# A decoder step on one core: the second layer norm's variance from sums taken per token during the mixing projection, and the modulated input as one product plus a low-rank matmul

## The chip, the cores and the metric

One Trainium2 chip; the program runs on 1 of its cores. The metric is device microseconds of one execution, as the median of several runs. The profile is of one further execution, in which a hardware profiler recorded every instruction. Engine names are those of the profile: PE (matmul), PEld (its weight loads), DVE (VectorE), ACT (ScalarE), POOL (GpSimd), SP (which issues the weight loads from memory). Each engine takes its own instructions strictly in the order in which the program wrote them, and an instruction that waits holds all those behind it on its engine.

## The reference

One layer for 288 tokens (256 of a prompt and 8 sequences of 4) with 2048 features. The change touches the stretch between the output projection of the mixing half and the up-projection of the channel half:

```
mod = silu(c) @ w_ada + b_ada
sh1, sc1, g1, sh2, sc2, g2 = split(mod, 6)
u   = layernorm(x) * (1 + sc1) + sh1
...                                   # convolution group and mLSTM group, concatenated into y
mix = y @ w_out
x   = layernorm(ALPHA * x + (1 + g1) * mix) * ln1_g + ln1_b
u2  = layernorm(x) * (1 + sc2) + sh2
a, g = split(u2 @ w_up, 2)
y   = silu(dwconv3(a)) * g
x   = layernorm(ALPHA * x + (1 + g2) * (y @ w_down)) * ln2_g + ln2_b
```

So two layer norms follow each other: the one that ends the mixing half, with gain ln1_g and bias ln1_b, and at once the one that opens the channel half. c has 9 rows: one for the prompt, one for each short sequence.

## The kernel before

**Layout.** Features lie on the 128 partitions and tokens along the free axis: an activation is 16 tiles (`xa[0]` to `xa[15]`) of 128x288. A weight matrix comes as 128x128 blocks, 16 to an item of 1 MB. ACT rounds each half of an item to `whi` and DVE subtracts to get `wlo` (helper `split_to`, L299 and L312); activations are split in the same way, and each product is three matmuls (`mm3`, L455 to L457). `next_block` asks for the half that is two halves ahead (`LOOK`). At most 7 items are held (`RAWB`).

**Items.** `plan` writes out the order of the items: weight items and, in between, items of `w_ada` that PE multiplies with silu(c) (`ada_item`, L366, tile `adaps`): 16 of them for each of the four vectors G1, SC2, SH2 and G2. The last vector, G2, is not needed before the down-projection; 13 of its items stand between the mixing projection and the up-projection, three later.

**Side work.** `side` starts a generator that is stepped by `tick`, once for each weight block; a `yield n` lets n blocks pass. It fixes the place of its instructions among the others on every engine at the time the program is built.

**Mixing projection.** Sixteen output tiles (tile `mix`, 48 matmuls each). The old `x` arrives by 16 loads that POOL issues one by one, each followed at once by a multiplication with ALPHA that waits for it (L1054 and L1055). After each tile `residual` (L1179 to L1183, DVE) adds the gated result. `TileNorm` with the name `ln1` takes the statistics of the first norm: after 11 tiles PE makes a shift from their sum, DVE and POOL subtract it, ACT squares, POOL adds up, and DVE adds up the tiles weighted with ln1_g (L1094).

**Between the projections.** Three matmuls with a matrix of ones give mean, mean square and weighted sum; then each tile is centred, scaled and squared again by DVE, POOL and ACT in an order that `Plan.run` works out from due times, and sixteen more matmuls (L1217, tile `var`) give the second variance. `rstd_of` (Ln and Exp on ACT, three DVE steps) gives the second scale. Then each tile is modulated (`u2_hi`, `u2_lo`), split, and used by the first six up-projection tiles (`pss`, 96 blocks).

**Later.** POOL brings `x1` back to its unscaled form beside the up-projection (`restore`, L1307 and L1308).

Of the kernel before, what the change touches and what calls it, by code (L numbers as in the profile page):

```python
# [36 lines left out]
U2_DVE = 2  # L37
SPLITS = (1, 3)
BIAS_AHEAD = 3
LN1_POOL = {1, 3, 5, 7, 9, 11, 13}  # L40
# [4 lines left out]
G2_EARLY = 13  # L45
G2_WAIT = 8
# [24 lines left out]
def plan():  # L71
# [66 lines left out]
    items += mix(rest[n:], w)  # L138
# [40 lines left out]
def constants():  # L179
# [17 lines left out]
    return dict(ident=ident, causal=causal, causal_s=causal_s, ind=ind, ind96=ind96, sel=sel, pick=pick)  # L197


def body(tc, d, off, items, blocks):  # L200
# [4 lines left out]
    with ctx:  # L205
# [50 lines left out]
        live = [0]  # L256
        barrier = [len(items)]
# [813 lines left out]
        class TileNorm:  # L1071


            def __init__(self, name, base, w=None):
# [5 lines left out]
                self.w = w  # L1080
                self.wsum = None

            def centre(self, m):
# [5 lines left out]
                if self.w is not None:  # L1089
                    if self.wsum is None:  # L1090
                        self.wsum = st(self.name + "w")
                        V.tensor_scalar(self.wsum, x, self.w[:, m:m + 1], None, ALU.mult)
                    else:
                        V.scalar_tensor_tensor(self.wsum, x, self.w[:, m:m + 1], self.wsum, ALU.mult, ALU.add)  # L1094
# [68 lines left out]
            def finish(self):  # L1163
# [25 lines left out]
        ngb = pers.tile([P, 1], F32, name="ngb")  # L1189
        V.tensor_scalar(ngb, gbm[:, 0:1], -1.0, None, ALU.mult)  # L1190
        bb1 = pers.tile([P, KB], F32, name="bb1")
        V.tensor_scalar(bb1, b1v, gbm[:, 1:2], None, ALU.subtract)

        ln1 = TileNorm("ln1", xa, g1v)
        for m in range(KB):
            ps = aps("mix")
            for k in range(KB):
# [4 lines left out]
            ln1.add(m, xa[m])  # L1202
        y = None
        steps = ln1.finish()
        drain(ada_done[len(GROUPS) + 1])
        drain(ada_done[len(GROUPS) + 2])
        x1 = xa
        var_ps = mps("var1", N)
        rstd1, mean = ln1.rstd, ln1.mean
        wp = st("wp")  # L1210
        done = []

        def scaled(E, k):
            E.tensor_tensor(x1[k], x1[k], rstd1, ALU.mult)
            q = st("sq1")
            A.activation(q, x1[k], AF.Square, bias=bb1[:, k:k + 1])
            T.matmul(var_ps, ones, q, start=(not done), stop=(len(done) == KB - 1))  # L1217
            done.append(k)

        next(steps)  # L1220
        pl = Plan()
        w = pl.op("v", VC, lambda E: V.scalar_tensor_tensor(wp, mean, ngb, ln1.psW, ALU.mult, ALU.add), at=0.6)
        r = ()
        for i in range(3):
            r = (pl.op("v", VC, lambda E: next(steps), deps=r, wait=LAT, at=0.9, stage=9),)
        pend = []
        for k in range(KB):
            e, c = ("g", GC) if k in LN1_POOL else ("v", VC)
            a = pl.op(e, c, lambda E, k=k: E.tensor_tensor(x1[k], x1[k], mean, ALU.subtract))
            b = pl.op("v", VC, lambda E, k=k: V.scalar_tensor_tensor(x1[k], x1[k], g1v[:, k:k + 1], wp,  # L1230
                                                                  ALU.mult, ALU.subtract),
                      deps=(a, w), wait=LAT)
            pend.append((k, e, c, b))
        for k, e, c, b in pend:
            pl.op(e, c, lambda E, k=k: scaled(E, k), deps=(b,) + r, wait=LAT, stage=1)
        pl.run()
        ln1 = None
        barrier[0] = len(items)
        var = st("var1")
        V.tensor_scalar(var, var_ps, EPS, None, ALU.add)  # L1240
        while items[pos[0]][0] == "a":
            take()
        rstd = rstd_of(var, "rstd1")

        def biased(k):
            A.activation(x1[k], x1[k], AF.Identity, bias=bb1[:, k:k + 1])

        for k in range(U2_DVE, U2_DVE + BIAS_AHEAD):
            biased(k)
        A.preload_act_table(AF.Silu)  # L1250
        def conv_state(n):
# [4 lines left out]

        sf_next = conv_state(0)
        u2 = [None] * KB
        hold = {}
        pss = [aps("up") if i < 3 else mps("up", N) for i in range(KOUT)]  # L1260

        def u2_hi(k):
            t = st("u2t")
            if k < U2_DVE:
                V.scalar_tensor_tensor(t, x1[k], bb1[:, k:k + 1], rstd, ALU.add, ALU.mult)
            else:
# [267 lines left out]
```

## Time and profile before

| | |
|---|---|
| time, median of 3 runs | 1553.33 us (1552.72 to 1553.34) |
| the profiled execution's own time | 1552.51 us |
| its span in the trace | 1550.6 us |
| granted PE clock, mean over the span | 0.991 |
| PE busy | 1510.7 us, 97% |
| DVE / ACT / POOL busy | 938.4 / 592.5 / 293.5 us |
| chain that ended last, by engine | PE 89%, DVE 8%, issue 1%, ACT 1% |
| mixing projection, first to last matmul | 517.9 to 639.8 us |
| first six up-projection tiles | 675.3 to 718.2 us |

PE's share is an average over stages. The place that the change rewrites is short: between 639.8 us and 675.3 us no weight block of a projection is multiplied. A row of the trace's timeline gives the start in us from the span's start, the duration, the engine, the line of the code, the operation with output and input tiles and shapes, how many like it are merged, and in brackets how long the engine had been idle and what ended that.

### The profile page before, as it was taken

To read this page: it belongs to the slowest core of one execution; us is meant where nothing else is said; L and a number is where in the kernel's file an instruction comes from. 1 tells how busy PE (TensorE), PEld (TensorE's weight loads), DVE (VectorE), ACT (ScalarE), POOL (GpSimd) and SP (SyncE) were. 2 spreads that over 40 slices of the span, in tenths; PEclk is the share of its full clock that TensorE was granted. 3 is DMA by queue.
4 is the path that set the end of the run, shared out by engine and by line. 5 is a ranking of instruction groups with operands and counts; after the bars stand their busy time and mean duration, and the time that the engine had idled before them with its cause. 6 is when DMAs were issued, how large, how long until landed. Compare 5 with 4: busy or idle time off the path is not lost.

```text
span 1550.6 us, 28061 instructions
## 1 busy us (share of the span) xinstructions
PE 1510.7 (97%) x11692; PEld 1409.7 (91%) x11692; DVE 938.4 (61%) x1643; ACT 592.5 (38%) x877; POOL 293.5 (19%) x502
## 2 busy tenths in 40 slices
PE   8999999999999999989999999999999999999994
PEld 7988988888888888569999999999999999999994
DVE  5566566777764446887655545555555445555557
ACT  5533234422234323355443333344443334444334
POOL 2320005210112234534530000000000000000235
PEclk9999999999999999999999999999999999999997
DMA  9887777569899876765545444444445444444401
GB/s 390 326 348 289 296 272 271 191 224 338 329 373 322 296 291 242 315 248 198 190 180 190 171 163 167 160 163 164 165 171 187 163 163 163 164 163 167 163 29 61
DMA packets 49614, 343.72 MB, mean 222 GB/s; under 512 B 5872, under 2 KB 6384, under 8 KB 9040
## 3 DMA queue, kind: packets, MB, share of 16 engines
q1 hardware_dynamic: 46656, 329.08, 57.1%
q0 software_dynamic: 2688, 12.68, 2.1%
q8 instruction: 91, 1.49, 0.4%
q14 instruction: 35, 0.29, 0.0%
q10 hardware_dynamic: 144, 0.19, 0.0%
HBM read 329.61 MB, written 12.31 MB: 221 GB/s over the span
## 4 chain that ended last, share of the span: by engine, by line
PE 89%; DVE 8%; issue 1%; ACT 1%; POOL 0%; DMA 0%; SPq 0%; DVEq 0%; ACTq 0%; POOLq 0%
PE g L456 6%; PE a L455 6%; PE g L455 6%; PE a L456 6%; PE g L457 6%; PE a L457 6%; PE dn L457 5%; PE dn L455 5%; PE dn L456 5%; PE adaps L366 5%; PE h L455 5%; PE h L456 4%; PE h L457 4%; PE mix L455 2%; DVE wlo L312 2%; PE mix L456 2%
## 5 line engine op out<-in xcount | busy, mean ns | idle before, releaser
L299 ACT CAST whi<-raw 128x1024 fp32r<-128x1024 f32 x410 | 424.1, 1046 | 435.2 <-PE dn L457 160.4
L312 DVE TENSOR_TENSOR wlo<-raw,whi 128x1024 fp32r<-128x1024 f32 x410 | 508.0, 1254 | 59.3 <-ACT whi L299 58.8
L457 PE MATMUL dn<-y2h,whi 128*128 128x288 f32 x704 | 208.0, 295 | 0.0
L455 PE MATMUL dn<-y2l,whi 128*128 128x288 f32 x704 | 207.5, 295 | 0.0
L456 PE MATMUL dn<-y2h,wlo 128*128 128x288 f32 x704 | 207.0, 294 | 0.0
L456 PE MATMUL g<-u2h,wlo 128*128 128x288 f32 x656 | 194.5, 297 | 0.0
L455 PE MATMUL a<-u2l,whi 128*128 128x288 f32 x656 | 194.1, 296 | 0.0
L455 PE MATMUL g<-u2l,whi 128*128 128x288 f32 x656 | 194.0, 296 | 0.0
L457 PE MATMUL g<-u2h,whi 128*128 128x288 f32 x656 | 193.7, 295 | 0.0
L457 PE MATMUL a<-u2h,whi 128*128 128x288 f32 x656 | 193.4, 295 | 0.0
L456 PE MATMUL a<-u2h,wlo 128*128 128x288 f32 x656 | 193.2, 295 | 0.0
L455 PE MATMUL h<-ul,whi 128*128 128x288 f32 x512 | 156.3, 305 | 4.4 <-DVE ul L581 1.6
L456 PE MATMUL h<-uh,wlo 128*128 128x288 f32 x512 | 152.2, 297 | 0.0
L457 PE MATMUL h<-uh,whi 128*128 128x288 f32 x512 | 151.8, 296 | 0.0
L455 PEld LDWEIGHTS dn<-y2l,whi 128*128 128x128 f32 x704 | 132.3, 188 | 0.1
L1016 POOL COPY fnew<-hal 128x2 f32<-128x2 f32 x44 | 9.7, 220 | 648.0 <-ACT hal L1328 648.0
L457 PEld LDWEIGHTS dn<-y2h,whi 128*128 128x128 f32 x704 | 132.2, 188 | 0.0
L456 PEld LDWEIGHTS dn<-y2h,wlo 128*128 128x128 f32 x704 | 132.0, 188 | 0.1
L455 PEld LDWEIGHTS a<-u2l,whi 128*128 128x128 f32 x656 | 123.4, 188 | 2.5 <-issue 2.5
L456 PEld LDWEIGHTS a<-u2h,wlo 128*128 128x128 f32 x656 | 123.5, 188 | 0.0
L455 PEld LDWEIGHTS g<-u2l,whi 128*128 128x128 f32 x656 | 123.4, 188 | 0.0
L456 PEld LDWEIGHTS g<-u2h,wlo 128*128 128x128 f32 x656 | 123.3, 188 | 0.0
(392 smaller groups left out, 2926.1 us busy)
## 6 DMA issues: line engine op xcount, KB each, us to landing
raw<-wst SPq DMA_DIRECT2D x300, 1024.0 KB, 4.9
raw<-cst SPq DMA_DIRECT2D x8, 1024.0 KB, 5.4
cs_o<-raw POOLq DMA_DIRECT2D x8, 1024.0 KB, 10.8
xa<-xT POOLq DMA_DIRECT2D x16, 144.0 KB, 5.4
xin<-xT SPq DMA_DIRECT2D x5, 432.0 KB, 5.6
y_o<-yout SPq DMA_DIRECT2D x4, 432.0 KB, 2.4
cp_o<-cnew POOLq DMA_DIRECT2D x8, 128.5 KB, 6.8
raw<-wst SPq DMA_DIRECT2D x2, 512.0 KB, 13.9
```

What stands on the lines that cost most here:

```text
L299: A.copy(his[n], raws[i][:, hf * 1024:(hf + 1) * 1024])
L312: V.tensor_tensor(lo, r, hi.bitcast(F32), ALU.subtract)
L366: T.matmul(ps[32 * s:32 * s + 32, 0:n], csil[:, k, :], r[:, c0:c0 + n], start=(k == 0), stop=(k == 15))
L455: T.matmul(ps, hi, ul, start=start, stop=False)
L456: T.matmul(ps, lo, uh, start=False, stop=False)
L457: T.matmul(ps, hi, uh, start=False, stop=stop)
L1016: G.tensor_copy(dst[:, 0, :], hal[:, NP:NP + 2])
```

## The change

**Statistics.** All sums that the two norms need are taken while the mixing projection runs. With z the shifted tile, six sums over the features are needed per token: z, z², (ln1_g z)², and z weighted with ln1_g, with -2 ln1_g² and with 2 ln1_g times the centred bias. The shift comes from the first 4 tiles (`S1`) in place of 11. For each tile ACT makes two squares, DVE three weighted running sums (`accumulate`), POOL three plain ones (`gather`).

**Steps with tokens on partitions.** The running sums are the left operand of matmuls with a column of ones (`sums`), so that 128 tokens lie on partitions and the sums of all 288 tokens are a 128x3 array. Both variances, both scales and the coefficients are then worked out on 128x3 arrays (`sv`).

**u2.** It is written as x1 times one factor per feature and token, plus a product of a coefficient matrix (`cft`, from `coefficients`, made while the projection runs) with a matrix `tok` that holds per-token values in 27 rows and zeros and ones in others; both are split in two parts for precision. The factor is spread over the partitions by matmuls with the identity (`tokens`). The constant rows of `tok` are a new input, loaded by POOL and cast by ACT ahead of the mixing projection.

**Order.** 6 items of G2 (`G2_EARLY`) stand between the projections and 10 within the up-projection; the last 6 weight items of the mixing projection (`MIX_LAST`) have no w_ada item between them. The first half of the up-projection's weights is split during the last mixing tile (`UP_AT`), four of the six sums are taken there too (`SUMS_AT`). `restore` takes three POOL operations per tile in place of two.

```diff
-U2_DVE = 2
-SPLITS = (1, 3)
-BIAS_AHEAD = 3
-LN1_POOL = {1, 3, 5, 7, 9, 11, 13}
+S1 = 4
+G2_FIRST = 4
+CF_AT = 4
+SUMS_AT = 10
+UP_AT = 9
 LN2_ROLES = "vgvvgvgvvgvgvvvd"
 STORES = [(0,), (1, 2), (3, 4, 5), (6, 7, 8), (9, 10, 11), (12, 13, 14), (15,)]
 RES0 = 8
 RES1 = 12
-G2_EARLY = 13
-G2_WAIT = 8
+G2_EARLY = 6
+MIX_LAST = 6
...
-    items += mix(rest[n:], w)
+    items += mix(rest[n:], w[:-MIX_LAST]) + w[-MIX_LAST:]
...
+        bb1, gg, gbb, ngg2, gbb2, gs, ng = (gb[:, i] for i in range(7))
         V.tensor_scalar(bb1, b1v, gbm[:, 1:2], None, ALU.subtract)
-
-        ln1 = TileNorm("ln1", xa, g1v)
+        V.tensor_tensor(gg, g1v, g1v, ALU.mult)
+        V.tensor_tensor(gbb, g1v, bb1, ALU.mult)
+        V.tensor_scalar(ngg2, gg, -2.0, None, ALU.mult)
...
+        for j, v in enumerate((gg, gbb2, gb[:, 7])):
+            V.tensor_tensor(tmp3[:, j, 0:8], v[:, 0:8], v[:, 8:16], ALU.add)
+            for n in (4, 2, 1):
+                V.tensor_tensor(tmp3[:, j, 0:n], tmp3[:, j, 0:n], tmp3[:, j, n:2 * n], ALU.add)
+        ps = mps("gbm3", 3)
+        T.matmul(ps, ones, tmp3[:, :, 0], start=True, stop=True)
+        cst = pers.tile([P, 6], F32, name="cst")
+        V.tensor_copy(cst[:, 0:3], ps)
...
+        tok = st("tok", F32R)
+        t = st("tok0")
+        nc.gpsimd.dma_start(out=t, in_=d["tok"])
+        A.copy(tok, t)
+        tt = st("tt", F32R)
+        G.memset(tt.bitcast(F32), 0.0)
...
+        def squares(m):
+            q, p = st("ln1q"), st("ln1p")
+            A.activation(q, xa[m], AF.Square)
+            A.activation(p, xa[m], AF.Square, scale=g1v[:, m:m + 1])
+            return q, p
+
+        def stats(m):
+            q, p = squares(m)
+            z = xa[m]
+            for name, w in (("w", g1v), ("x", ngg2), ("b", gbb2)):
+                accumulate(name, z, w[:, m:m + 1])
+            acc1["n"] = m
+            gather("q", q)
+            gather("p", p)
+            gather("z", z)
+
+        def first_stats(total):
+            A.preload_act_table_set("natural_log_exp_and_others")
+            yield 4
+            ps = mps("shift1", N)
+            T.matmul(ps, ones, total, start=True, stop=True)
+            sh = st("shift1")
+            A.activation(sh, ps, AF.Copy, scale=2048.0 / (P * S1))
+            for m in range(S1, KB):
+                G.tensor_tensor(xa[m], xa[m], sh, ALU.subtract)
+            yield 1
+            for m in range(S1):
+                V.tensor_tensor(xa[m], xa[m], sh, ALU.subtract)
+                stats(m)
+                yield 2
...
+            F = rawp.tile([P, 2048], F32, tag="r", name=nm("cf"))
+            G.memset(F, 0.0)
...
+                A.copy(Cv[:, ks, 0:27], D[h][:, :, 0:27])
+                A.copy(Cv[:, ks, 96:105], D[h][:, :, 27:36])
+                A.copy(Cv[:, ks, 64:91], D[h][:, :, 0:27])
...
+                V.tensor_tensor(Cv[:, ks, 32:59], D[h][:, :, 0:27], F[:, ks, 0:27], ALU.subtract)
+                V.tensor_tensor(Cv[:, ks, 105:114], D[h][:, :, 27:36], F[:, ks, 96:105], ALU.subtract)
...
+            for q in range(4):
+                ps = mps("cft")
+                for k in range(4):
+                    T.transpose(ps[:, k * P:(k + 1) * P], F[:, 4 * q + k, :], ident)
+                for k in range(2):
+                    t = st("cft", F32R)
+                    A.copy(t[:, 0:256], ps[:, 256 * k:256 * k + 256])
...
+            for i, (a, b) in enumerate(BLK):
+                T.matmul(stp[bank][:, 8 * i + c:8 * i + c + w], x[:, a:b], rhs, start=start and i == 0,
+                         stop=stop and i == 2)
+
+        def late_sums():
+            yield SUMS_AT
+            for name, c in (("w", 1), ("x", 2), ("b", 3), ("p", 5)):
+                sums(name, acc1[name], c)
+
+        def up_split():
+            yield UP_AT
+            barrier[0] = len(items)
+            split_to(upcoming_w())
...
+            elif m < KB - 1:
+                if m == S1:
+                    drain(fs)
+                stats(m)
...
-        steps = ln1.finish()
-        drain(ada_done[len(GROUPS) + 1])
-        drain(ada_done[len(GROUPS) + 2])
-        x1 = xa
-        var_ps = mps("var1", N)
-        rstd1, mean = ln1.rstd, ln1.mean
-        wp = st("wp")
-        done = []
-
-        def scaled(E, k):
-            E.tensor_tensor(x1[k], x1[k], rstd1, ALU.mult)
-            q = st("sq1")
-            A.activation(q, x1[k], AF.Square, bias=bb1[:, k:k + 1])
-            T.matmul(var_ps, ones, q, start=(not done), stop=(len(done) == KB - 1))
-            done.append(k)
...
+        q, p = squares(KB - 1)
+        sums("z", acc1["z"], 0)
+        sums("q", acc1["q"], 4)
+        sums("lin", xa[KB - 1], 0)
+        sums("q", q, 4, True)
+        sums("p", p, 5, True)
...
+        V.tensor_tensor(Rr, r1, r2, ALU.mult)
+        r2b = sv[:, :, 10:11].to_broadcast([P, 3, 27])
+        V.tensor_tensor(tt[:, :, 0:27], tp3, r2b, ALU.mult)
+        V.tensor_tensor(tt[:, :, 32:59], tp3, r2b, ALU.mult)
+        V.tensor_tensor(tp3, tp3, r2b, ALU.mult)
+        V.tensor_tensor(tt[:, :, 64:91], tp3, ttf[:, :, 0:27], ALU.subtract)
...
+        for _ in range(G2_FIRST):
+            if items[pos[0]][0] == "a":
+                take()
+        rps = mps("rr", N)
+        tokens(rps, spread(11), P)
+        R = st("R")
+        A.copy(R, rps)
+        tps = mps("tokp", N)
+        tokens(tps, lambda i: ttf[:, i, 0:96], 96)
+        A.copy(tok[0:96], tps[0:96])
...
+        def u2_t(k):
+            t = st("u2t")
+            V.scalar_tensor_tensor(t[:, 0:NP], x1[k][:, 0:NP], gs[:, k:k + 1], R[:, 0:NP], ALU.mult, ALU.mult)
+            V.tensor_tensor(t[:, NP:N], x1[k][:, NP:N], R[:, NP:N], ALU.mult)
+            V.tensor_tensor(smp(t), smp(t), bc_t(fsv[:, k]), ALU.mult)
+            hold[k] = t
+        def u2_corr(k):
+            cps[k] = mps("corr", N)
+            T.matmul(cps[k], cft[k // 2][:, (k % 2) * P:(k % 2 + 1) * P], tok, start=True, stop=True)
...
+            V.tensor_tensor(t, t, cps.pop(k), ALU.add)
...
+        for k in range(KB):
+            for i, p in enumerate(pss):
+                mm3(p, next_block(), u2[k], k == 0, k == KB - 1)
+                if i == KOUT // 2 - 1 and k + 2 < KB:
+                    u2_corr(k + 2)
+                    u2_hi(k + 2)
+                    if k + 3 < KB:
+                        u2_t(k + 3)
+                    u2_lo(k + 2)
...
+                G.tensor_tensor(x1[k], x1[k], rb[0], ALU.mult)
+                G.tensor_tensor(x1[k], x1[k], rb[1], ALU.subtract)
+                G.tensor_scalar(x1[k], x1[k], ga[:, 0, k:k + 1], ga[:, 1, k:k + 1], ALU.mult, ALU.add)
```

The order of the built program shows the change at three places. The numbers in the names count buffers. First, ACT at the start of the mixing projection, before: the gate of the last o tile (`sg`), its split (`yh`), then weight halves.

```order
L299 CAST whi_5996<-raw_5828 128x1024
L1064 ACTIVATE sg_6013<-o_5935 128x288
L462 CAST yh_6016<-sg_6013 128x288
L299 CAST whi_6046<-raw_5828 128x1024
L299 CAST whi_6076<-raw_5900 128x1024
```

And ACT at the same place now, where `tok` is the new table and `whi_6009` and `whi_6096` are the two weight halves of the second mixing tile:

```order
L312 CAST whi_6009<-raw_5885 128x1024
L1077 ACTIVATE sg_6026<-o_5961 128x288
L475 CAST yh_6029<-sg_6026 128x288
L1228 CAST tok_6069<-tok_1032_6070 128x288
L312 CAST whi_6096<-raw_5885 128x1024
L312 CAST whi_6126<-raw_5966 128x1024
```

One instruction is new on ACT: the cast of the loaded table stands ahead of the second tile's second weight half. The load that it reads is on POOL's queue; POOL, from the last two of the 16 loads of x on, now:

```order
L1067 DMA xa_5407<-xT 128x288
L1068 TENSOR_SCALAR xa_5407<-xa_5407 128x288
L1067 DMA xa_5410<-xT 128x288
L1068 TENSOR_SCALAR xa_5410<-xa_5410 128x288
L1227 DMA tok_1032_6070<-tok 128x288
L1230 MEMSET tt_6073 128x288
L1375 COPY total_6147<-xa_5365 128x288
```

Before, the copy for the sum of the tiles followed the last load's multiplication directly; now the table's load and a memset stand between them, behind all 16 loads.

Second, DVE where the shift has just been made. Before, after the eleventh mixing tile (`ln1shift`; `wlo_6900` is a weight half of a later tile):

```order
L1086 TENSOR_TENSOR xa_5365<-xa_5365,ln1shift_6825 128x288
L1092 TENSOR_SCALAR ln1w_6851<-xa_5365,small 128x288
L1086 TENSOR_TENSOR xa_5368<-xa_5368,ln1shift_6825 128x288
L1094 SCALAR_TENSOR_TENSOR ln1w_6851<-xa_5368,small,ln1w_6851 128x288
L1086 TENSOR_TENSOR xa_5371<-xa_5371,ln1shift_6825 128x288
L1094 SCALAR_TENSOR_TENSOR ln1w_6851<-xa_5371,small,ln1w_6851 128x288
L1179 SCALAR_TENSOR_TENSOR xa_5398<-mix_6799,mod,xa_5398 128x256
L1182 TENSOR_TENSOR rs_6890<-mix_6799,mod 128x32
L1183 TENSOR_TENSOR xa_5398<-xa_5398,rs_6890 128x32
L312 TENSOR_TENSOR wlo_6900<-raw_6696,whi_6862 128x1024
```

Now, during and after the fifth mixing tile (`mix_6366`), from the fourth shifted tile on; `wlo_6519` is the first weight half of the seventh mixing tile:

```order
L1285 TENSOR_TENSOR xa_5374<-xa_5374,shift_1074_6394 128x288
L1246 SCALAR_TENSOR_TENSOR aw_6416<-xa_5374,small,aw_6416 128x288
L1246 SCALAR_TENSOR_TENSOR ax_6418<-xa_5374,gb,ax_6418 128x288
L1246 SCALAR_TENSOR_TENSOR ab_6420<-xa_5374,gb,ab_6420 128x288
L1180 SCALAR_TENSOR_TENSOR xa_5377<-mix_6366,mod,xa_5377 128x256
L1183 TENSOR_TENSOR rs_6499<-mix_6366,mod 128x32
L1184 TENSOR_TENSOR xa_5377<-xa_5377,rs_6499 128x32
L1246 SCALAR_TENSOR_TENSOR aw_6416<-xa_5377,small,aw_6416 128x288
L1246 SCALAR_TENSOR_TENSOR ax_6418<-xa_5377,gb,ax_6418 128x288
L1246 SCALAR_TENSOR_TENSOR ab_6420<-xa_5377,gb,ab_6420 128x288
L325 TENSOR_TENSOR wlo_6519<-raw_6300,whi_6481 128x1024
```

Each tile has three weighted sums behind its shift where it had one. Between the shift matmul and `wlo_6519` DVE now has four subtractions, fifteen weighted sums, one weight half and one residual; `wlo_6900` before had three subtractions, three weighted sums and one residual ahead of it.

Third, PE between the two projections. Before, from the last mixing matmul (seven more w_ada items, the sixteen matmuls of `var` and four further w_ada items follow behind these rows):

```order
L457 MATMUL mix_7156<-yh_6016,whi_7107 128x288
L366 MATMUL adaps_7237<-raw_6898,csil 32x512 x4
L1138 MATMUL ln1B_7045<-ln1q_6849,ones 128x288
L1141 MATMUL ln1A_7044<-ln1xs_7171,ones 128x288
L1142 MATMUL ln1A_7044<-xa_5410,ones 128x288
L1143 MATMUL ln1B_7045<-ln1q_7234,ones 128x288
L1173 MATMUL ln1W_7254<-ln1w_6851,ones 128x288
L366 MATMUL adaps_7237<-raw_6945,csil 32x512 x4
```

Now, from the sums behind the last mixing tile:

```order
L1345 MATMUL stat_7386<-ones,az_6438 128x1 x3
L1345 MATMUL stat_7386<-ones,ln1q_6412 128x1 x3
L1345 MATMUL stat_7386<-w_6043,xa_5410 128x4 x3
L1345 MATMUL stat_7386<-ones,ln1q_7427 128x1 x3
L1345 MATMUL stat_7396<-ones,ln1p_7428 128x1 x3
L379 MATMUL adaps_7479<-raw_6871,csil 32x512 x4
L379 MATMUL adaps_7479<-raw_6922,csil 32x512 x4
L379 MATMUL adaps_7479<-raw_6963,csil 32x512 x4
L379 MATMUL adaps_7479<-raw_7036,csil 32x512 x4
L1444 MATMUL rr_7504<-small,sv 128x128 x2
L1444 MATMUL rr_7504<-small,sv 128x32
L1444 MATMUL tokp_7510<-small,tt_6073 96x128 x2
```

The sixteen `var` matmuls are gone, the matmuls for the sums have one or four columns, and six w_ada items (four here, two a little later) stand where thirteen did.

More of the change, by code (lines that the diff above doesn't have):

```diff
@@ L271, in load @@
         def load():
-            while emitted[0] < len(items) and live[0] < RAWB:
+            while emitted[0] < len(items) and live[0] < RAWB - held[0]:
                 i = emitted[0]
@@ new lines, in body, with sums @@
+        stp = {}
+        def sums(name, x, c, stop=False):
+            bank = c // 5
+            start = bank not in stp
+            if start:
+                stp[bank] = mps("stat", 24)
+            w = 4 if name == "lin" else 1
+            rhs = w4 if name == "lin" else ones[:, 0:1]
+            for i, (a, b) in enumerate(BLK):
[5 more added lines that the diff above has]
+                sums(name, acc1[name], c)
@@ L1220, in body @@
[L1220 to L1237, printed above, removed]
-        barrier[0] = len(items)
[L1239 to L1249, printed above, removed]
+            if m < S1:
+                if m == 0:
+                    total = st("total")
+                    G.tensor_copy(total, xa[0])
+                else:
+                    G.tensor_tensor(total, total, xa[m], ALU.add)
+                if m == S1 - 1:
+                    fs = side(first_stats(total))
+                    fs[0] = next(fs[1])
+                    total = None
+            elif m < KB - 1:
+                if m == S1:
+                    drain(fs)
+                stats(m)
@@ new lines, in body @@
+        s1 = newton_steps(r1, var1, t2)
+        next(s1)
+        V.scalar_tensor_tensor(wp, mean, nEg, wv, ALU.mult, ALU.add)
+        V.scalar_tensor_tensor(xv, mean, Eg2, xv, ALU.mult, ALU.add)
+        V.scalar_tensor_tensor(bv, mean, nEgb2, bv, ALU.mult, ALU.add)
+        V.tensor_tensor(xv, xv, mean, ALU.mult)
+        for _ in s1:
+            pass
+        V.tensor_tensor(xv, xv, S5[:, :, 5], ALU.add)
+        V.tensor_tensor(t1, wp, wp, ALU.mult)
+        V.tensor_tensor(xv, xv, t1, ALU.subtract)
@@ new lines, in body @@
+        V.tensor_tensor(xv, xv, r1, ALU.mult)
+        V.tensor_tensor(xv, xv, bv, ALU.add)
+        V.tensor_tensor(xv, xv, r1, ALU.mult)
+        V.tensor_scalar(v2, xv, Ebb2, EPS, ALU.add, ALU.max)
+        s2 = newton_steps(r2, v2, t2)
+        next(s2)
+        V.tensor_tensor(MWr, MW, sv[:, :, 8:9].to_broadcast([P, 3, 2]), ALU.mult)
+        for i in range(2):
+            V.tensor_tensor(tp3[:, :, 9 * i:9 * i + 9], tmask, sv[:, :, 12 + i:13 + i].to_broadcast([P, 3, 9]),
+                            ALU.mult)
@@ new lines, in body, with tokens @@
+        for _ in s2:
+            pass
+        V.tensor_tensor(Rr, r1, r2, ALU.mult)
[4 more added lines that the diff above has]
+        V.tensor_tensor(tt[:, :, 64:91], tp3, ttf[:, :, 0:27], ALU.subtract)
+        def tokens(ps, lhs, n):
+            for i, (a, b) in enumerate(((0, P), (P, NP), (NP, N))):
+                T.matmul(ps[0:n, a:b], lhs(i), ident[:, P - (b - a):P], start=True, stop=True)
```

193 lines of the change are left out of this document (139 added, 54 removed).

## The prediction

> **What bounds the kernel now.** I read the page's head first, then a table of stretches around the place that the change rewrites, then PE's timeline there.
>
> ```profile
> span 1550.6 us, 28061 instructions
> 640.00:650.00 10.00, 10.00 (x79) 3.93 (x82) 8.00 (x15) 2.03 (x5) 5.29 (x6) 1.00 0.73 266
> 650.00:660.00 10.00, 6.05 (x24) 2.50 (x16) 10.00 (x16) 4.48 (x9) 6.25 (x7) 1.00 1.00 422
> 660.00:670.00 10.00, 9.09 (x36) 3.78 (x40) 7.53 (x16) 5.27 (x12) 2.86 (x3) 0.83 0.66 274
> 670.00:680.00 10.00, 6.28 (x40) 4.95 (x33) 8.76 (x18) 5.02 (x8) 2.57 (x3) 0.83 0.99 397
> 676.00:680.00 4.00, 4.00 (x21) 4.00 (x21) 2.94 (x9) 1.50 (x3) 0.00 (x0) 0.57 1.01 428
> 740.00:760.00 20.00, 20.00 (x153) 20.00 (x152) 13.21 (x18) 8.98 (x13) 13.52 (x16) 1.00 0.52 184
> ```
>
> Columns: stretch, length, then busy time of PE, PEld, DVE, ACT and POOL, granted clock, DMA share, GB/s. In a steady stage (740 to 760 us) PE issues 153 matmuls in 20 us, 0.131 us each: a block of three takes 0.394 us, a mixing tile of 48 takes 6.3 us. PE is the bound there; between 650 and 680 us it isn't: DVE fills whole slices, and PE does other things.
>
> ```profile
> 639.99 1.06 PE L366 MATMUL adaps<-raw,csil 128*32 128x512 f32 x8
> ...
> 643.60 7.08 PE L366 MATMUL adaps<-raw,csil 128*32 128x512 f32 x64
> ...
> 667.96 3.64 PE L366 MATMUL adaps<-raw,csil 128*32 128x512 f32 x32
> 675.32 0.40 PE L455 MATMUL up<-u2l,whi 128*128 128x288 f32 x1 [3.72 <-DVE u2l L1280]
> ...
> 718.43 1.06 PE L366 MATMUL adaps<-raw,csil 128*32 128x512 f32 x8
> ```
>
> The mixing projection's last matmul ends at 640.0 us, the first up matmul starts at 675.3: a gap of **35.3 us**. Inside it PE does 8+64+32 records, 13 w_ada items of 8, at 7.08/8 = 0.885 us each. The first six up tiles last from 675.3 to 718.4, **43.1 us**, where 288 matmuls need 37.8. After its idle 3.7 us PE got a clock of 0.57 for 4 us, a loss of 1.7 us.
>
> **The gap after the change.** Its start is read from how the last tile ends now; its steps are priced from short DVE and ACT instructions elsewhere in this trace.
>
> ```profile
> 310.88 0.16 DVE L856 SCALAR_TENSOR_TENSOR sc<-sc 128x1 f32<-128x1 f32 x1
> 311.08 0.16 DVE L857 TENSOR_TENSOR sc<-sc,colP 128x1 f32<-128x1 f32 x1
> L474 ACT ACTIVATE mvt<-mvt 128x9 f32<-128x9 f32 x1 | 0.2, 218 | 6.6 <-DVE mvt L910 6.6
> L1250 ACT ACT_TABLE_LOAD x1 | 1.3, 1283 | 0.0
> 640.16 0.48 DVE L1179 SCALAR_TENSOR_TENSOR xa<-mix,mod,xa 128x256 f32<-128x256 f32 x1 [4.33 <-PE mix L457]
> 651.37 0.30 PEld L1217 LDWEIGHTS var<-sq,ones 128*128 128x128 f32 x2 [1.60 <-ACT sq L1216]
> 634.53 0.77 PE L389 MATMUL adatp<-small,adat 128*128 128x128 f32 x4 [0.68 <-DVE adat L381]
> ```
>
> Counted from the last mixing matmul: the residual is ready after 0.9 us and ACT's two squares after 1.9. PE takes 15 sums of two passes each; a pass is a weight load, of which the row has two in 0.30, the second 0.11 behind the first; I take 0.13 a pass, so the first norm's sums are done at 3.5 and the last at 4.2. DVE then goes step by step at 0.20 us a dependent step (310.88 to 311.08): four steps, Ln and Exp on ACT (0.22 each), three steps, seven steps, Ln and Exp, three steps and one: 18 x 0.20 + 4 x 0.22 is 4.5 with the overlaps of independent ones taken off at 0.3, so the scale stands at 7.7. Four w_ada items (3.5 us) lie beside it on PE. Six short matmuls and two ACT copies (0.4 each) bring the factor at 9.1 and `tok` at 10.0; the ACT table load, queued behind, ends at 11.3 and holds the first rounding of u2; then rounding 0.4, DVE's subtraction 0.45. PE can start at **12.3 us**. The bounds are 10 (the table load hidden, loads at 0.11) and 16 (every overlap lost). Taken 12.3: **-23.0 us**.
>
> The up tiles: DVE's work per input tile (one product, two short ones, one sum, one difference, three quarters of a weight half) falls a little under PE's 2.5 us, POOL leaves the stage, and PE gets 16 more matmuls of 0.131 (14 of them inside). Between 39.8 (PE alone) and 43.1 (as now) I take 41.3, and 1.6 for six matmuls behind it that spread two rows for `restore`: **-0.2**.
>
> Seven w_ada items leave the gap and are met again within the up-projection, each alone. What one alone costs shows in the mixing stage, where every tile has one:
>
> ```profile
> 524.62 0.48 DVE L1179 SCALAR_TENSOR_TENSOR xa<-mix,mod,xa 128x256 f32<-128x256 f32 x1 [3.22 <-PE mix L457]
> ...
> 532.17 0.48 DVE L1179 SCALAR_TENSOR_TENSOR xa<-mix,mod,xa 128x256 f32<-128x256 f32 x1 [4.47 <-PE mix L457]
> ```
>
> 7.55 us a tile less 6.31 is 1.24 an item: **+8.7**. In the mixing stage four items now stand in pairs, which saves 4 x 0.36: **-1.4**. `restore`'s third operation per tile lies on POOL beside the up-projection, where POOL was busy 13.5 of 20 us and has 4.7 us a tile: nothing; with that cover gone it would be 16 us at the first down tile.
>
> **The mixing stage: two new holds.** These are what the diff's words don't tell.
>
> First, the table `tok`. ACT casts it ahead of the second weight half of the second mixing tile, and POOL issues its load behind the 16 loads of x, each of which POOL waits for.
>
> ```profile
> 520.82 1.37 POOL L1055 TENSOR_SCALAR xa<-xa 128x288 f32<-128x288 f32 x1 [4.15 <-DMA xa<-xT]
> 522.14 0.59 POOL L1054 DMA_DIRECT2D xa<-xT  x1
> ...
> 554.77 0.92 POOL L1055 TENSOR_SCALAR xa<-xa 128x288 f32<-128x288 f32 x1 [4.21 <-DMA xa<-xT]
> 555.65 1.41 POOL L1155 COPY ln1sum<-xa 128x288 f32<-128x288 f32 x1
> 528.97 1.05 ACT L299 CAST whi<-raw 128x1024 fp32r<-128x1024 f32 x1 [3.32 <-PE mix L457]
> xa<-xT POOLq DMA_DIRECT2D x16, 144.0 KB, 5.4
> y_o<-yout SPq DMA_DIRECT2D x2, 144.0 KB, 2.0
> sffn<-sffn POOLq DMA_DIRECT2D x2, 120.0 KB, 2.8
> ```
>
> The last loads here are number 11 (its multiplication at 520.8) to 16 (554.8), 37 us into the mixing projection, and nothing in the change lets them start earlier. PE wants the held half 8 blocks and one item behind the first tile's end: 524.5 + 1.0 + 3.15 = 528.6, where ACT's own row stands, and 2.7 later for the three w_ada items that now come earlier: **531.3**. With ACT held no weight half is made, items stop being freed, and the memory queue empties: a load then lands in 2.0 (the 144 KB row of `y_o`) to 2.8 us, not 5.4. I take 3.9 for the next load (the traffic is still running out) and 2.7 for the others: from 522.1, one load at 3.9 + 0.92, four at 2.7 + 0.92, the table 2.7, its cast 0.43, the weight half 1.05 and 1.22 make 546.8. PE is held for **15.5 us** (10 with all at 2.0; 30.5 with all at 5.4), and 1.7 more for the clock, by the row of 676 to 680: **+17.2**. The longer start of the stage (PE now waits about 5 us for a second small sum, behind 23 short DVE steps) falls into this wait.
>
> The Trainium skill, "DMA: Bandwidth & Descriptors", section on the anatomy of one DMA, gives a fixed 2.0 us and 436 GB/s for a load issued by GpSimd, so an estimate of 2.34 us for one of x; by it the hold would end at 543.4, and the sum come out 3.5 us lower. The trace's 5.4 us is more than twice that, with other transfers in the way; no row here has such a load on an empty queue.
>
> Second, DVE when the shift comes: 4 tiles wait for it, and each takes a subtraction and three weighted sums ahead of the next weight half.
>
> ```profile
> 604.14 4.58 POOL L1106 TENSOR_TENSOR xa<-xa,ln1shift 128x288 f32<-128x288 f32 x5 [1.33 <-ACT ln1shift L1104]
> 605.29 0.80 DVE L1092 TENSOR_SCALAR ln1w<-xa,small 128x288 f32<-128x288 f32 x1
> 606.01 1.07 DVE L1086 TENSOR_TENSOR xa<-xa,ln1shift 128x288 f32<-128x288 f32 x1
> 607.11 0.95 DVE L1094 SCALAR_TENSOR_TENSOR ln1w<-xa,small,ln1w 128x288 f32<-128x288 f32 x1
> 607.99 1.05 DVE L1086 TENSOR_TENSOR xa<-xa,ln1shift 128x288 f32<-128x288 f32 x1
> ...
> 612.27 0.52 DVE L1094 SCALAR_TENSOR_TENSOR ln1w<-xa,small,ln1w 128x288 f32<-128x288 f32 x1
> ...
> 615.42 1.82 DVE L312 TENSOR_TENSOR wlo<-raw,whi 128x1024 fp32r<-128x1024 f32 x1
> ```
>
> While POOL subtracts too, DVE's subtraction steps at 1.10 us and a weighted sum at 0.88; with POOL quiet at 612.27 the sum takes 0.52. POOL now has 12 subtractions (11 us) and then 12 sums queued, so I take the slow rates. From the shift matmul: 1.3 to the first DVE step; first tile 3.3, second 3.7, a weight half 1.75, third and fourth 3.7 each, a residual 0.75, three sums 2.65, the next half 1.8: ready at 22.7. PE wants it after 0.5 + 5.1 (rest of the tile) + 1.24 + 6.3 + 1.24 = 14.4. PE waits **8.3 us**, plus 1.7 for the clock: **+10.0**. At bare rates (0.44 to 0.52 an operation) it would be ready at 12.5: nothing.
>
> Smaller: 16 transposes of 0.13 and their four entries (row 634.53), **+2.4**; 24 weight-load passes for the four early sums, **+3.4**; these sums' wait for DVE's and POOL's last additions, 0 to 3, taken **+1.0**; the cleared coefficient tile and its casts, which stand on ACT ahead of a weight half of tile 13, 0 to 3, taken **+2.0**.
>
> Sum: -23.0 - 0.2 + 8.7 - 1.4 + 17.2 + 10.0 + 2.4 + 3.4 + 1.0 + 2.0 = +20.1 on the profiled execution's 1552.5 (its span and 1.9 around it): 1572.6. The median of the runs is 0.8 above that execution: **1573**.
>
> **The rivals.**
>
> 1. *The cast doesn't hold ACT.* It would take the table to be in place by about 528 us, so that POOL is through its loads 27 us earlier than in the trace. Then 17.2 goes: 1556 as a median, 0.2% above before, so about no change; with DVE's bare rates too, 1546, and faster. It decides when the sixteenth load lands before 526. Against it: the rows at 520.8 and 554.8, and six landings can't fit into 9 us even at 2.0. For it: what I read off two queues has never run. 17%.
> 2. *The loads keep their pace of 5.4.* The hold is 30.5, and the time 1588. For it: that is what all 16 do now (median); against it: the weight items stop. 14%.
> 3. *DVE's burst runs at bare rates.* Nothing is lost at the seventh tile: 1563. For it: rows as at 612.27 stand between slow ones; against it: POOL's queue is never empty there. 15%.
>
> The forecast itself gets 52%; 2% is left for the gap staying much longer than 16 us.
>
> **How the numbers follow.** About 0.2% is what a measurement of this kernel can tell from no change. Rival 1 is split into faster 11%, same 4% and slower 2%; with odd ends of the others: faster 0.11, same 0.06, slower 0.83. The range goes from 1551 (part of rival 1) to 1590 (past rival 2).
>
> **What would show it.** In the changed kernel's trace ACT's idle time in front of the cast of `tok`, ended by a DMA, some 20 us long, and PE idle in the second mixing tile until about 547 us; a PE wait for `wlo` at the seventh tile's first half; a gap of 12 us from the last mixing matmul to the first up matmul; a first six up tiles of 41 us. It is wrong if the cast of `tok` starts before 530, or if PE's idle time in the mixing stage is under 10 us.

## The result and the profile after

The changed kernel takes **1577.18 us** (median of 4 runs, 1573.77 to 1579.28), the kernel before, measured beside it, 1553.03: a ratio of 1.0151, 95% interval 1.0139 to 1.0163. The profiled execution is the shortest of the four (1573.77, span 1572.0), and the forecast's sum for it was 1572.6; the forecast median, 1573, lies 4.2 us under the measured one.

The first rows are the longest entries of the list of what PE waited for from 500 to 760 us (sum, times, longest); `gbm` at L1217 is the second small sum, `cft` the transposes of the coefficients, `stat` the sums. Then comes PE's timeline at the borders of the stages.

```profile
PE mix L469 <- DVE wlo L325: 6.3, 2, 6.1
PE gbm L1217 <- DVE gbt L1215: 5.3, 1, 5.3
PE cft L1325 <- DVE cf L1320: 5.0, 1, 5.0
PE stat L1345 <- POOL ln1p L1256: 3.1, 1, 3.1
PE mix L468 <- ACT whi L312: 2.4, 1, 2.4
PE adaps L379 <- issue: 1.7, 1, 1.7
```
```profile
526.17 0.59 PE L1217 MATMUL gbm<-gbt,ones 128*128 128x3 f32 x2 [5.25 <-DVE gbt L1215]
526.69 1.94 PE L379 MATMUL adaps<-raw,csil 128*32 128x512 f32 x8
528.56 0.61 PE L468 MATMUL mix<-yl,whi 128*128 128x288 f32 x1
...
536.74 1.93 PE L379 MATMUL adaps<-raw,csil 128*32 128x512 f32 x16
...
580.66 0.40 PE L468 MATMUL mix<-yl,whi 128*128 128x288 f32 x1 [2.45 <-ACT whi L312]
587.11 0.61 PE L469 MATMUL mix<-yh,wlo 128*128 128x288 f32 x1 [6.06 <-DVE wlo L325]
...
675.82 0.30 PE L470 MATMUL mix<-yh,whi 128*128 128x288 f32 x1
679.50 5.04 PE L379 MATMUL adaps<-raw,csil 128*32 128x512 f32 x32
688.85 0.29 PE L468 MATMUL up<-u2l,whi 128*128 128x288 f32 x1
730.05 0.29 PE L470 MATMUL up<-u2h,whi 128*128 128x288 f32 x1
733.20 0.41 PE L468 MATMUL a<-u2l,whi 128*128 128x288 f32 x1
```

Before, PE's only wait within the projection was one of 0.7 us. The borders give an account of the two spans that closes:

| stretch of PE | before | after | difference |
|---|---|---|---|
| start of the span to the first mixing matmul | 517.9 | 528.6 | +10.7 |
| mixing projection | 122.2 | 147.6 | +25.4 |
| gap to the first up matmul | 35.3 | 12.7 | -22.5 |
| six up tiles, and to the next tile's first matmul | 44.1 | 44.4 | +0.2 |
| the rest | 831.2 | 838.8 | +7.6 |
| span | 1550.6 | 1572.0 | +21.4 |

The gap shrank as the change has it. In front of it 36.1 us were added. The wait for ln1p has a row of ACT's ahead of it, in the last tile but one:

```profile
666.00 1.04 ACT L312 CAST whi<-raw 128x1024 fp32r<-128x1024 f32 x1 [8.47 <-DMA raw<-wst]
```

ACT was idle until a weight load landed; its squares and POOL's sum of ln1p come after it, and PE's wait of 3.1 us ends with that sum. One row answers the forecast's main term, from ACT's timeline, and three of POOL's belong to it.

```profile
537.69 0.43 ACT L1228 CAST tok<-tok 128x288 fp32r<-128x288 f32 x1 [15.48 <-DMA tok<-tok]
538.03 2.95 ACT L312 CAST whi<-raw 128x1024 fp32r<-128x1024 f32 x3
```
```profile
531.82 0.59 POOL L1067 DMA_DIRECT2D xa<-xT  x1
534.36 0.92 POOL L1068 TENSOR_SCALAR xa<-xa 128x288 f32<-128x288 f32 x1 [1.95 <-DMA xa<-xT]
535.24 0.60 POOL L1227 DMA_DIRECT2D tok<-tok  x1
```

ACT is held for 15.48 us behind the sixteen loads, as foretold; but PE begins the second tile only when its two w_ada items end (the row at 536.74), at 538.6, reaches the held half 3.15 later, at 541.7, and doesn't wait there at all. So one of the forecast's signs failed (PE idle in the second tile until about 547 us), its largest term, 17.2 us, cost nothing in this execution, and the sum came out right all the same. The experiments had to say why.

### The profile page after: what moved, and what is told of

The parts are those of the page before. It is cut to its first block, busy times and chain, and to the rows that moved or that the text cites. A ratio compares the mean times of both kernels' runs of the same rounds, so it can differ in the third digit from the quotient of the medians.

```text
span 1572.0 us, 28298 instructions
## 1 busy us (share of the span) xinstructions
PE 1516.0 (96%) x11762; PEld 1418.8 (90%) x11762; DVE 954.4 (61%) x1707; ACT 588.1 (37%) x878; POOL 306.7 (20%) x516
## 4 chain that ended last, share of the span: by engine, by line
PE 88%; DVE 7%; ACT 1%; issue 1%; DMA 1%; POOL 0%; SPq 0%; DVEq 0%; ACTq 0%; POOLq 0%
PE adaps L379 6%; PE g L468 5%; PE a L468 5%; PE g L469 5%; PE g L470 5%; PE dn L470 5%; PE a L469 5%; PE dn L468 5%; PE a L470 5%; PE dn L469 5%; PE h L468 5%; PE h L469 4%; PE h L470 4%; PE mix L468 2%; DVE wlo L325 2%; PE mix L469 2%
## 5 line engine op out<-in xcount | busy, mean ns | idle before, releaser
L325 DVE TENSOR_TENSOR wlo<-raw,whi 128x1024 fp32r<-128x1024 f32 x410 | 514.5, 1270 | 72.1 <-ACT whi L312 71.2
L470 PEld LDWEIGHTS g<-u2h,whi 128*128 128x128 f32 x656 | 123.4, 188 | 0.0
```

Of the source, the lines that this page charges most:

```text
L325: V.tensor_tensor(lo, r, hi.bitcast(F32), ALU.subtract)
L470: T.matmul(ps, hi, uh, start=False, stop=stop)
```

## Does the cast of `tok` hold PE, or the small sum ahead of it?

Four kernels: the changed one again (`again`); the cast placed behind the third tile (`tok_late`); the second small sum placed behind the first tile (`gbm_late`); both (`both_late`).

```diff
-        A.copy(tok, t)                                        # tok_late
+        tok0 = t
...
+            if m == 2:                                        # behind residual(xa[m], ps, G1, m)
+                A.copy(tok, tok0)
...
-        ps = mps("gbm3", 3)                                   # gbm_late: with its copies into cst
-        T.matmul(ps, ones, tmp3[:, :, 0], start=True, stop=True)
...
+            if m == 0:                                        # behind residual
+                ps = mps("gbm3", 3)
+                T.matmul(ps, ones, tmp3[:, :, 0], start=True, stop=True)
```

> The changed kernel once more. Its four runs lay between 1573.8 and 1579.3 us, the profiled one lowest, and there the last load of x landed at 534 us and ACT's cast of tok cost PE nothing. Theory T (the cast holds PE only where the loads of x land late, and that is the spread): a profile with a longer time shows the sixteenth load later than 537 us and PE idle in the second mixing tile by about the difference. Theory F (the forecast: the cast is the largest loss, 17 us, always): PE idle there by over 10 us in this profile. Rival R (the spread is from elsewhere): the time is longer by 3 us or more with PE never idle in the second tile. Median 1577 by all.

> The changed kernel with ACT's cast of tok moved from ahead of the second tile's weight halves to behind the third tile's residual; its load stays where it is. F: 17 us less, 1560. T: 0 to 4 us less, 1573 to 1577, with less spread between its runs, since only the slow runs lose time at the cast. In the profile ACT is not idle for 15 us in front of a cast, and whi stands early, by both.

> The changed kernel with the second small sum (gbm3) and the copies out of it moved behind the first mixing tile, so that PE has no idle time of 5.25 us ahead of the first tile. If that wait is a loss by itself (T1): 5.3 of wait and some 2.5 of low clock go, 8 us less: 1569. If the cast of tok then takes its place (T2: PE reaches the held weight half some 8 us earlier, at about 534, while tok lands at about 538): only 3 to 4 us less, 1573 to 1574, and PE idle in the second tile for 4 to 6 us, ended by ACT. F has T2's sign, with PE held until the cast, so 0 to 1 us less.

> Both moves, the cast of tok and the second small sum. T: 8 us and what the cast costs in the slow runs, 1566 to 1569, PE without idle time up to the fifth tile. F: 17 and 8 together less, 1552. If T2 holds in the kernel with the sum alone moved, this one is 4 to 5 us below that.

| | median, us | runs | ratio to before (95%) |
|---|---|---|---|
| `again` | 1577.56 | 1577.39 to 1581.43 | 1.0164 (1.0146 to 1.0181) |
| `tok_late` | 1574.98 | 1574.32 to 1576.19 | 1.0140 (1.0123 to 1.0157) |
| `gbm_late` | 1580.15 | 1574.44 to 1583.36 | 1.0170 (1.0145 to 1.0196) |
| `both_late` | 1569.28 | 1567.53 to 1572.67 | 1.0107 (1.0089 to 1.0125) |

Each move alone gives little or nothing (-2.6 and +2.6 us against `again`, with intervals that overlap); together they give 8.3. Once the other move is made, moving the cast is worth 10.9 us and moving the sum 5.7. Two waits lay one over the other. The rows are from PE's timeline of `again` (two) and of `gbm_late`, then ACT's of `gbm_late`, then its stretches (length; busy time of PE, PEld, DVE, ACT, POOL; granted clock, DMA share, GB/s).

```profile
540.91 0.40 PE L468 MATMUL mix<-yl,whi 128*128 128x288 f32 x1 [0.83 <-ACT whi L312]
542.17 0.40 PE L469 MATMUL mix<-yh,wlo 128*128 128x288 f32 x1 [0.86 <-DVE wlo L325]
```
```profile
544.84 0.61 PE L468 MATMUL mix<-yl,whi 128*128 128x288 f32 x1 [11.89 <-ACT whi L312]
```
```profile
543.41 0.43 ACT L1222 CAST tok<-tok 128x288 fp32r<-128x288 f32 x1 [21.96 <-DMA tok<-tok]
```
```profile
534.00:544.00 10.00, 0.00 (x0) 0.00 (x0) 0.00 (x0) 0.59 (x2) 4.06 (x7) 0.60 0.14 44
```

In `again` the table landed 1.8 us later than in the first profile, and PE waited 0.83 and 0.86 in the second tile; its span was 3.6 us longer. That is part of the spread between runs of the changed kernel. In `gbm_late` PE reached the held half nearly 9 us earlier than in the first profile, at 532.9, and stood there for 11.89: the forecast's mechanism, at its place, in full view. It had PE there at 531.3 and the table landed at 544.1; here the cast begins at 543.4. The loads of x were later than in the first profile: the thirteenth was issued at 527.2 and not at 518.2 (528.5 in the kernel before). It shows in the times too: the runs of `gbm_late` lie 9 us apart, those of `tok_late` 2.

A load on the emptied queue is the other thing to read here. In `gbm_late` the queues move 44 GB/s while PE is stopped, which is three loads of 144 KB in 10 us and nothing else. There `tok` takes 2.3 us from its issue to its landing; in the first profile it takes 2.4, and the three loads of x ahead of it 2.5, 2.8 and 2.5. The forecast took 2.7. The Trainium skill, "DMA: Bandwidth & Descriptors", section on the anatomy of one DMA, gives a fixed 2.0 us and 436 GB/s, so an estimate of 2.34 us: the trace agrees for `tok`, and the loads of x lie 0.2 to 0.5 above it.

`x_ahead` removes the cause and leaves the cast where the change put it: POOL issues each load three ahead of its scaling and doesn't wait for each landing (with the sum moved as in `gbm_late`).

```diff
             nc.gpsimd.dma_start(out=t, in_=xd[:, m])
-            G.tensor_scalar(t, t, ALPHA, None, ALU.mult)
             xa.append(t)
+            if m >= 3:
+                G.tensor_scalar(xa[m - 3], xa[m - 3], ALPHA, None, ALU.mult)
+        for t in xa[KB - 3:]:
+            G.tensor_scalar(t, t, ALPHA, None, ALU.mult)
```

> The kernel with the second small sum moved (gbm_late, 1580 us, PE 11.9 us idle in the second tile), the cast of tok where the change has it, and POOL issuing the loads of x three ahead of the scaling, so that it doesn't wait for each landing. If POOL's one-by-one loads are what makes tok late (T): the sixteenth load lands by about 505 us, tok before 515, no wait at the cast, and the time is that of both moves or 1 to 2 us less, 1567 to 1569. Rival: the loads wait for free buffers and not for each other, tok still lands at 538 to 545, and the time stays at 1578 to 1580.

It took 1567.91 us (ratio 1.0095, 1.0080 to 1.0110), 12 less than `gbm_late`, and PE no longer waits in the second tile. From POOL's timeline:

```profile
484.86 1.77 POOL L1072 TENSOR_SCALAR xa<-xa 128x288 f32<-128x288 f32 x1 [0.72 <-DMA xa<-xT]
510.95 0.60 POOL L1224 DMA_DIRECT2D tok<-tok  x1 [24.32 <-PE adatp L402]
```

The last load is scaled at 484.9 and not at 534, and ACT casts the table at 524.5 without a wait. The loads had waited for each other, not for buffers, and the cast was late only because of them.

## The seventh tile, and the two short waits behind it

In the first profile PE's wait of 2.45 us at the seventh tile is ended by ACT and its 6.06 by DVE, but both are DVE's burst. ACT's weight half stands behind two squares that wait for DVE's fourth subtraction; from ACT's timeline:

```profile
578.80 0.44 ACT L1260 ACTIVATE ln1q<-xa 128x288 f32<-128x288 f32 x1 [3.05 <-DVE xa L1285]
579.58 1.03 ACT L312 CAST whi<-raw 128x1024 fp32r<-128x1024 f32 x1
```

Three kernels, each with both moves in it, so beside 1569.28.

```diff
-                yield 2                                       # spread: DVE's catch-up, one of 4 tiles at a time
+                yield 10
...
-                if m == S1:                                   # spread and lin4
-                    drain(fs)
...
-                stats(m)                                      # lin4
+                q, p = squares(m)
+                gather("q", q)
+                gather("p", p)
...
+            yield 6
+            for m in range(S1):
+                sums("lin", xa[m], 0)
+                yield 2
...
-            for name, c in (("w", 1), ("x", 2), ("b", 3), ("p", 5)):     # cf_p: p is summed in the tail
+            for name, c in (("w", 1), ("x", 2), ("b", 3)):
...
+        sums("p", acc1["p"], 5)
...
-            yield 6                                           # cf_p: ahead of the transposes
+            yield 14
```

> Both moves (1569.3 us) and DVE's catch-up for the four early tiles spread: 10 blocks between two of them and not 2, and tiles 5 on no longer wait for its end. There PE waits 2.4 + 6.1 us now and has a low clock behind it. Theory O (only the order is bad, DVE has room later): the wait goes, 10 us less, 1559. Theory D (DVE has no room: from the fifth tile to the eleventh it is busy some 75 of 79 us, its 16 us of catch-up fit nowhere): the wait moves to later tiles, 0 to 4 us less, 1565 to 1569.

> Both moves (1569.3 us), and the weighted sums of the four early tiles taken by PE (three short products of two passes a tile, as the last tile has them) and not by DVE; DVE keeps their subtraction alone. Theory D: 12 of DVE's operations (some 11.6 us at 0.97) go, the wait of 8.5 and its low clock of 1.7 go, PE gets 4 x 0.72 = 2.9: 7 us less, 1562. Theory O, that only the order counts: the same or less gain, since four subtractions still stand together: 1562 to 1566, with a wait for wlo of 2 to 4 us left. If it falls by less than 3 us, neither is right and the wait has another cause.

> Both moves (1569.3 us), 14 blocks and not 6 between the coefficient table's last DVE step and its transposes, and the sum of ln1p taken with the tail's sums and not ahead of the last tile's end. T: the wait of 5.0 us for cf goes with about 1 of low clock, and the wait of 3.2 for ln1p with 2.2 of low clock, less 0.7 in the tail: 10 us less, 1559. Rival (the waits hide the load of the last weight item, for which ACT is idle 8.5 us at 666 and which starts only when the table's buffer is free, now 3 us later): PE waits for that weight half in the last tile, 4 to 6 us less, 1563 to 1565.

`spread` took 1563.84 us (ratio 1.0062, 1.0046 to 1.0078), `lin4` 1562.49 (1.0056, 1.0041 to 1.0071), `cf_p` 1559.47 (1.0042, 1.0028 to 1.0057): 5.4, 6.8 and 9.8 less. (The kernel before, measured beside these three, took 1.1 us more than beside `both_late`; by the ratios it is 7.0, 7.9 and 10.1.) `cf_p` and `lin4` came within 0.5 us of what was expected, though in `cf_p` 1.8 us of the wait for the coefficient tile are left, and a new one of 0.6 for `az`; `spread` lies between its two theories. Stretches of `both_late`, then of `lin4`:

```profile
560.00:580.00 20.00, 11.62 (x84) 9.09 (x82) 19.82 (x22) 6.29 (x11) 20.00 (x21) 0.90 0.41 170
580.00:600.00 20.00, 19.70 (x127) 17.10 (x128) 16.18 (x24) 6.78 (x11) 10.50 (x9) 0.84 0.81 315
```
```profile
560.00:580.00 20.00, 20.00 (x144) 17.99 (x143) 15.66 (x18) 9.13 (x17) 19.46 (x20) 0.92 0.75 281
580.00:600.00 20.00, 20.00 (x153) 17.39 (x152) 17.19 (x20) 7.07 (x10) 11.19 (x10) 1.00 0.75 304
```

With the catch-up on DVE, DVE has 19.8 busy of 20 us, POOL all 20, and PE 11.6. With the weighted sums of four tiles on PE, DVE has room, and from 560 to 610 us PE stands still for nothing. (Ahead of that it waits 4.4 us for the shift, where POOL adds up behind its late loads; in `x_ahead` that wait is gone.)

## All of it together

`all_lin4` joins `x_ahead`, `lin4` and `cf_p` (with 18 blocks ahead of the transposes); `all_spread` has `spread` in place of `lin4`.

> All mendings in one: x loaded three ahead, the second small sum behind the first tile, PE's short products for the four early tiles, the sum of ln1p in the tail, and 18 blocks ahead of the transposes. If the losses are separate waits (T): from 1568 with the first two, 7 less for the four tiles, 10 less for the table and ln1p, 1 to 2 more for the 4 further blocks: 1549 to 1551, 0.1 to 0.3% below the kernel before, and PE idle for less than 3 us from the first mixing tile to the last. Rival (they cover one another, as the cast and the small sum did): 1554 or more, with a new wait that is named by the profile.

> The same, but with DVE's catch-up spread over the tiles and not handed to PE. Spread alone left a wait of 2.4 us for wlo and no added work on PE, against 2.9 us of added products: 1550 to 1552. If a wait of DVE grows again because the tiles now come earlier and closer (Theory D), 1554 or more.

`all_lin4` took **1547.82 us** (1547.65 to 1550.27), 0.9968 of the kernel before (0.9956 to 0.9981), 1 to 3 us less than expected. `all_spread` took 1554.54 (1.0011, 1.0002 to 1.0020), as its rival, theory D, had it. PE's longest waits from 500 to 670 us, `all_lin4` (four) and then `all_spread` (two):

```profile
PE adaps L379 <- issue: 1.7, 1, 1.7
PE corr L1494 <- DVE u2t L1498: 0.7, 2, 0.5
PE stat L1349 <- DVE xa L1183: 0.7, 1, 0.7
PE mix L469 <- DVE wlo L325: 0.6, 1, 0.6
```
```profile
PE mix L469 <- DVE wlo L325: 5.0, 4, 2.4
PE stat L1343 <- DVE xa L1183: 2.5, 1, 2.5
```

Once PE isn't stopped elsewhere, DVE has no room for all of its catch-up: it is busy for 19.8 of 20 us from 560 to 580 and again from 580 to 600, the wait for `wlo` comes back at four places, and the last residual is late. That the gain of `spread` came out of time that other waits gave it fits this, but wasn't tried by itself. So the seventh tile's wait is DVE's load, and not the order of its work alone.

`best` adds two small things to `all_lin4`: the gathered sum of ln1p stands ahead of the last tile's own sums, and the ten lone w_ada items come as five pairs.

> all_lin4 (1547.8) with two small mendings: the gathered sum of ln1p stands ahead of the last tile's own sums, where PE waited 0.66 us for the residual, and the ten w_ada items that were met one by one beside the up-projection are met in five pairs. Theory P (an item alone costs more than one in a pair, as 1.24 against 0.885 in the gap of the trace before): 5 x 0.2 to 0.36 less, and 0.6 for the sum: 1545.4 to 1546.2. Rival: the lone items cost no more there, 1547.2, or pairs hold the weight loads up, 1548 or more.

1546.57 us (1545.92 to 1549.26), 0.9960 of before (0.9947 to 0.9974). The wait of 0.7 us ahead of the last tile's sums is gone, and the profiled span is 1.7 us shorter than that of `all_lin4`, as expected from both parts. But the median lies 0.4 above the expected 1545.4 to 1546.2, and the intervals of the two kernels overlap, so the step between them isn't established by the times.

## A clock that falls though PE shows as busy

In the tail of all these kernels the w_ada items run at half clock with hardly a wait ahead of them (after: 32 matmuls in 5.04 us, where 0.885 an item makes 3.5). PE has just done 30 short passes (36 in `all_lin4`); in the first profile the clock was 1.00 from 677 to 679 us, during them, and 0.50 from 679 to 681. `short_passes` puts 72 more into the middle of the projection.

```diff
+            if m == 8:
+                probe = mps("probe", 24)
+                for i in range(12):
+                    for j, (a, b) in enumerate(BLK):
+                        T.matmul(probe[:, 8 * j:8 * j + 4], y[0][0].bitcast(F32)[:, a:b], w4, start=i == 0 and j == 0,
+                                 stop=i == 11 and j == 2)
```

> all_lin4 with 36 more short products (four columns wide, two passes each, 72 passes, some 8.4 us) on PE in a row behind the ninth mixing tile, added work whose result isn't used. In the tail of these kernels the granted clock falls to 0.5 with PE never idle for more than 0.7 us. Theory S (a row of short passes lowers the granted clock as idle time does): the clock in the windows behind the passes falls below 0.8 for some 4 us, and the time rises by 8.4 + 2 = 10 us or more. Rival I (only PE's idle time does it, and the tail's fall comes from its short waits): the clock stays 1.00 and the time rises by 8.4 at most, less what DVE's waits give back.

It took 1564.05 us (two runs; ratio 1.0068, 1.0050 to 1.0087), 16 more than `all_lin4`. Stretches of 2 us, from the passes' start at 594.5 (columns as above):

```profile
594.00:596.00 2.00, 2.00 (x20) 2.00 (x19) 1.19 (x4) 0.36 (x2) 0.00 (x0) 1.00 0.61 197
596.00:598.00 2.00, 2.00 (x15) 2.00 (x15) 2.00 (x4) 1.45 (x3) 1.77 (x2) 0.72 0.81 340
598.00:600.00 2.00, 2.00 (x11) 2.00 (x11) 2.00 (x2) 0.00 (x0) 1.89 (x2) 0.50 0.00 0
...
608.00:610.00 2.00, 2.00 (x10) 0.58 (x3) 0.00 (x0) 0.00 (x0) 0.00 (x0) 0.50 0.00 0
610.00:612.00 2.00, 2.00 (x15) 2.00 (x14) 0.00 (x0) 0.00 (x0) 0.00 (x0) 0.86 0.61 188
612.00:614.00 2.00, 2.00 (x17) 2.00 (x16) 0.00 (x0) 0.54 (x1) 0.00 (x0) 1.00 1.01 426
```

PE shows as busy in every stretch, PEld as long as the passes last (to 607.6), and the clock falls to 0.50 within 4 us and stays there until some 3 us after the passes. That is theory S: such a row lowers the clock with no idle time in the trace. Which part of it does so isn't shown (the four columns, the form with two passes, or the share of weight loads), and as the profile only models the ends of matmuls, a PE that shows as busy may do little. Four rows of six passes with 0.75 us of full matmuls between them, in `all_lin4`, did not lower it (its clock is 1.00 from 560 to 580 us).

## Why the forecast's sum held and its largest term didn't

The sum held by luck. First, four rows of the changed kernel's gap:

```profile
682.68 0.17 DVE L1434 TENSOR_TENSOR sv<-sv 128x3 f32<-128x3 f32 x1
684.48 0.86 PE L1444 MATMUL rr<-small,sv 128*128 128x128 f32 x6
686.39 1.28 ACT L1459 ACT_TABLE_LOAD   x1
687.69 0.43 ACT L1490 CAST u2h<-u2t 128x288 fp32r<-128x288 f32 x1
```

- **The gap: right in size, half right in mechanism.** -23.0 forecast, -22.5 measured; PE starts 12.7 us after the last mixing matmul, and 12.3 was given. Its end is as worked out: the table load holds the first rounding of u2, whose input stood at 687.3. Its middle isn't: DVE had the scale after 6.7 us and not 7.7, but the four w_ada items that were to lie beside it took 5.04 in place of 3.5, at the low clock, so PE came to the factor's matmuls 1.6 us after the scale. The two errors nearly cancel.
- **Up tiles, lone items:** 41.3 and 1.6 forecast, 41.5 and 1.9 measured; +8.7 forecast for seven items, +7.6 measured for the rest of the span, 1.09 each if all of it is theirs.
- **DVE's burst: right.** 8.3 of wait and 1.7 of clock forecast at the seventh tile's first half; 0.23 (a tile earlier) + 2.45 + 6.06 measured, and the 47 matmuls behind it took 7.86 in place of 6.2. Rival 3 (bare rates) is out: DVE's weighted sums there took 0.80 to 1.06 us, about as assumed.
- **The cast of `tok`: right mechanism, wrong overlap in this kernel.** It was priced at 15.5 + 1.7. Two steps failed. First, the time at which PE wants the held half was put at 531.3, with the sentence that the longer start "falls into this wait". It is the other way round: the wait for the second small sum (5.25 us, 0.6 for its matmuls, and some 2.5 of low clock: the item took 1.94, the first tile 8.25 in place of 6.6) comes first, and with a w_ada item ahead of which PE waited 1.67 it brings PE to the held half at 541.7. Second, the loads of x were 10 us ahead of the kernel before already when the queue emptied (the thirteenth issued at 518.2 and not at 528.5), and `tok` landed at 537.7 and not at 544.1; the price of a load on the emptied queue, 2.7, was near (2.4 to 2.8). (The 2.0 taken as the least was the time of a store, and the second sum given beside the first is 3.4 lower by its terms, not 3.5.) So the cover decided, not the hold: without that sum ahead of it the hold cost 11.9 us (`gbm_late`). In the median of the changed kernel the cast costs 2.6 (`tok_late`), though the intervals of the two overlap.
- **The smaller terms: two right, two too small.** 24 passes were put at 3.4 and took 3.5, the transposes at 2.4 and took 3.2 in all. The clear and casts of the coefficient tile were put at 2.0; PE waited 5.0 for DVE's last step on it, and ran some 1 us slow behind it. The late sums' wait was put at 1.0; it was 3.1, and the next 21 matmuls took 5.06 in place of 2.8, most of them at a clock of 0.50. That the weight load ahead of it was late since the coefficient tile holds one of the item buffers is argued from the rows, not tried.
- **The sum.** The cast gave 17.2 too much; the start (10.7, of which only the items' 2.7 were priced, and 1.6 of low clock in the first tile), the coefficient tile and the late sums gave some 18 back. 1572.6 against 1573.77 is the balance of these errors: luck, not proof of the terms.
- **Rivals.** Rival 1 (1556) had its condition wrong and its effect right for one execution: the cast didn't hold PE, though it was as late as 537.7. Rival 2 is out, by the loads of 2.4 to 2.8 on the emptied queue.

Open: the 1.7 us that PE waits ahead of a w_ada item at 505 us, for nothing that the profile names, in the changed kernel and in every one made from it. It wasn't tried.

## What to carry to other kernels

Two waits on one path are not two terms: the first to come covers the second, and taking one away brings the other out, so price them together and test them together. When a forecast's total is right, set its terms beside a stage account that closes before believing it. An instruction put "early, since it is only a cast" holds its whole engine behind the slowest queue that feeds it (15.48 us here, and 21.96 in `gbm_late`).

## What was not expected of the hardware

In `short_passes` a row of short passes halves the granted clock while PE shows as busy (0.72 and 0.50 within 4 us of its start, 1.00 again some 3 us behind its end), so 72 of them cost 16 us, where 8.4 was their price at full clock. And 16 loads of 144 KB, issued three ahead, were through in 34 us (by 485) where one by one they took 86 (until 534), beside the weight loads.
